# Token sums by halves, a first block in halves, no products that open banks early, and new ranks in the planner of a hybrid attention and pooling layer

## The chip, the cores and the metric

The kernel runs on one core of one Trainium2 chip. The metric is device microseconds (us) of one execution. The parts of the core are called by the profile's names: PE is TensorE, PEld its weight loads, DVE is VectorE, ACT is ScalarE, POOL is GpSimd, SP issues DMAs.

## The reference, cut to what matters

One decoder layer on 1024 tokens with 1024 channels, in float32:

```python
mod = silu(c) @ w_ada + b_ada
shift, scale, gate = jnp.split(mod, 3, axis=-1)
h = rms_norm(x, norm_w) * (1.0 + scale) + shift
proj = h @ w_in
u_pool, g_pool, q, k, v, g_attn, qi, ki, wi = jnp.split(proj, split_points, axis=-1)
pool_out = pool_mixer(u_pool, w_pool, pool_scale) * silu(g_pool)   # windows 2, 4, 8, 16
q = rope(rms_norm(q, q_norm_w)); k = rope(rms_norm(k, k_norm_w))
qi = rope(qi); ki = rope(ki)
score = sum over heads of relu(qi . ki) * wi, causal               # index scores
attn_out = attention of q over its 256 best scored keys * silu(g_attn)
x = x + gate * (concat([pool_out, attn_out]) @ w_out)
```

## The kernel before

The work is tiled by 128: 8 blocks of 128 channels, 8 tiles of 128 tokens. A float32 product of h with weights is made of three products of rounded parts: `hhi` with `wh`, `hhi` with `wl`, `hlo` with `wh`, where `wh` and `hhi` are the rounded values and `wl` and `hlo` what the rounding left.

The order on every engine is set when the kernel is built. `hybrid_layer` holds some 40 generators ("strands"), one for each piece of work; each yields an operation (`Op`), several to be issued together (`Group`), or the same operation on two or three engines to choose from (`Either`). `Flow.run` keeps a model of the engines' clocks, and issues at each step the operation whose modelled wait plus rank is least: the ranks stand in the table `EARLY` (for PE in `LAST`), `SAFE` adds a margin ahead of products of a strand, `_cost`, `HOP` and their like are the model's durations, `ROOM`, `KEEP`, `MIX`, `QK` and `IK` say how many buffers or banks a strand leaves to others. Since `Op.issue` (line 196) issues every instruction, every row of the profile has line 196, and rows are told apart by tiles.

The lead, which the change rewrites:

- `token_sums` (line 482) loads x as 8 blocks `xt`, squares each on ACT (`sq`), adds some of them on DVE, and sums the squares over channels with 64 products `m<-c,sq` of one column each, into eight columns of one bank.
- `token_scales` (line 534) takes the square root on ACT, the reciprocal on DVE, and spreads the result over the partitions by 8 PE transposes `m<-c,c` into two banks `ps_b`, copied by ACT to `rsb`.
- `modulations` (line 584) makes two DVE passes over 128x1024 weights (`wa`) for each block j; the sum of each goes through a small step, a DVE `TENSOR_SCALAR` on 128x1, that gives `gs` (the gear) and `mod_sb` (the shift).
- `h_block(j)` (line 608) makes xn, `hhi` on ACT and `hlo`. Block 0 takes xn on DVE in halves from `ps_b`; blocks 1 to 7 take it on POOL from `rsb`, and ACT applies gear and shift.
- `lead_line` (line 663) is PE's first long piece: for each j the index queries, three kinds of product, each with 512 and with 256 columns. It opens two banks with one float32 product each, `mm(acc..., ident, xt[7])`, the rows `m<-xt,c`.

After the lead come the key and value rows, then the steps of `ORDER`: a (gates), q (queries), m (pooling mixers); at "|" they wait for four finished score tiles. Beside these run the index scores, and then the selection of the 256 best keys by bisection: for tiles 2, 3 and 4 on DVE (31 steps; each step counts with one `junk` for each tile and moves the bound with `aq` and `xq`; `yq` is on POOL), for tiles 5, 6 and 7 on ACT (`ajunk`). Mixer g makes window sums `nx` from u, then u itself, which PE multiplies (`m<-u,c`), then `gp`, and its parts `mph` and `mpl` for the output projection. `attention` takes maxima `mx` of the products `m<-kT,qr` on DVE and goes on with exponentials, transposes and products; `project_pooled` and `project_attended` end the kernel.

Of the kernel before, what the change touches and what calls it, by code (L numbers as in the profile page):

```python
# [38 lines left out]
EARLY = {"main": 0.6, "fill": 0.4, "weights": 0.0, "evac": -1.0, "side": 0.2, "h": -0.2, "mods": -0.2,  # L39
         "select": -0.1, "scores": -0.6, "attend": -1.1, "late": 1.0, "kv": -0.3, "qi": -0.8, "pick": -0.6,  # L40
         "mix": -0.36, "rotated": -0.18, "query_loads": 0.01, "exps": -0.11, "score_sums": -1.13,
         "key_value_out": -0.58, "index_queries": -1.39, "norm": -2.29, "gate_loads": -0.03, "token_scales": -0.31,
         "gate_mods": 0.58, "unit": -0.41, "index_scores": -0.39, "lead_loads": 1.53, "out": -1.53, "lead_out": -0.72,
         "weight_loads": -0.1, "key_value_weights": -0.24, "main_line": 1.04, "output_line": 0.3, "turns": -1.82,
         "finish": -0.62, "index_keys": -0.9, "h_block": -0.1, "attention_keys": -0.68, "turned": -1.72,
         "h_blocks": -0.05, "gated": -1.24}
# [22 lines left out]
PW_POOL = 0.4  # L69
XO_POOL = 0.45  # L70
BACK = 0.5
SPAN = 0.5
# [1448 lines left out]
```

## Time and profile before

| | us |
|---|---|
| runs of the kernel | 533.91, 534.77, 534.86 (median 534.77) |
| profiled execution, its time | 535.14 |
| profiled execution, its span | 533.2 |
| PE busy | 510.2 (96%) |
| DVE busy | 427.3 (80%) |
| ACT busy | 376.4 (71%) |
| POOL busy | 160.5 (30%) |

The span runs from the first to the last instruction; what lies around it is 1.9 us. A busy share is a mean over stages: the table of stretches shows where an engine is full. A row of a timeline gives start, duration, engine, operation, out<-in, count, and in brackets the idle time just before it with the engine that ended it. Several rows of one kind that follow each other are one row with a count.

### The profile page before, as it was taken

The page shows a single profiled execution, that of the slowest core. Times are in us where ns is not written, and L with a number is a line of the kernel's source. Part 1 is how long each engine was busy: PE and PEld are TensorE (multiplying, and loading weights), DVE is VectorE, ACT ScalarE, POOL GpSimd, SP SyncE. Part 2 cuts the span into 40 slices and gives each one's busy share as a digit, 9 for nine tenths or more (in the row PEclk, how much of TensorE's full clock was granted, in tenths as well). Part 3 has the DMA queues.
Part 4 walks back from the last instruction along what each step waited for, and adds up shares of the span by engine and source line. Part 5 has one row for each costly group of instructions (what it writes and reads, how often), then busy time and mean ns, then how long its engine had stood idle before and what let it go on. Part 6 is the DMA issues. An engine that isn't in the chain of part 4 may idle for free.

```text
span 533.2 us, 7630 instructions
## 1 busy us (share of the span) xinstructions
PE 510.2 (96%) x2492; PEld 378.2 (71%) x2492; DVE 427.3 (80%) x895; ACT 376.4 (71%) x848; POOL 160.5 (30%) x173
## 2 busy tenths in 40 slices
PE   5969999999999999999999797999999999999997
PEld 5758899755657887878878575876585856636575
DVE  0699996699886899999999899798856999886142
ACT  6357731487878888999962789799999834796420
POOL 1298240000000345555246147243202423100000
PEclk9979999999999999999999798899999999999999
DMA  8995418202011111121110014465252723301044
GB/s 307 405 408 167 136 48 297 79 0 80 21 61 59 41 41 41 39 71 49 36 44 20 21 60 125 131 188 182 69 177 81 227 90 100 98 20 41 1 157 158
DMA packets 28023, 58.29 MB, mean 109 GB/s; under 512 B 3792, under 2 KB 7888, under 8 KB 27984
## 3 DMA queue, kind: packets, MB, share of 16 engines
q1 hardware_dynamic: 27984, 57.81, 31.8%
q8 instruction: 19, 0.31, 0.3%
q14 instruction: 20, 0.16, 0.1%
HBM read 47.32 MB, written 10.49 MB: 108 GB/s over the span
## 4 chain that ended last, share of the span: by engine, by line
PE 55%; DVE 31%; ACT 6%; issue 5%; DMA 1%; POOL 1%; SPq 0%; DVEq 0%; POOLq 0%
PE m L196 55%; DVE junk L196 9%; ACT ex L196 4%; DVE ex L196 3%; DVE selw L196 3%; DVE aq L196 2%; DVE nx L196 1%; DVE sw L196 1%; DVE xq L196 1%; DVE key L196 1%; DVE wa L196 1%; DVE u L196 1%; DVE hlo L196 1%; DVE qr L196 1%; DVE gp L196 1%
## 5 line engine op out<-in xcount | busy, mean ns | idle before, releaser
L196 PE MATMUL m<-hhi,wh 128*128 128x512 f32 (+1 forms) x320 | 120.8, 399 | 0.5 <-ACT hhi L196 0.5
L196 PE MATMUL m<-hlo,wh 128*128 128x512 f32 (+1 forms) x320 | 114.8, 383 | 4.5 <-DVE hlo L196 4.5
L196 PE MATMUL m<-hhi,wl 128*128 128x512 f32 (+1 forms) x320 | 115.7, 383 | 0.0
L196 ACT ACTIVATE ajunk<-key,xq 128x768 bf16<-128x768 uint16 (+2 forms) x93 | 96.4, 1037 | 4.9 <-DVE xq L196 3.6
L196 PEld LDWEIGHTS m<-hhi,wh 128*128 128x128 f32 x320 | 59.6, 191 | 21.0 <-issue 7.4
L196 POOL TENSOR_TENSOR wl<-ld,wh 128x512 fp32r<-128x512 f32 x40 | 61.6, 1542 | 33.8 <-ACT wh L196 15.3
L196 PEld LDWEIGHTS m<-hlo,wh 128*128 128x128 f32 x320 | 59.2, 190 | 16.9 <-DVE hlo L196 5.2
L196 DVE TENSOR_SCALAR_CACHE_REDUCE junk<-key,xq 128x384 bf16<-128x384 uint16 (+2 forms) x93 | 69.1, 743 | 2.2
L196 PEld LDWEIGHTS m<-hhi,wl 128*128 128x128 f32 x320 | 59.5, 191 | 12.9 <-issue 1.9
L196 ACT ACTIVATE ex<-ex,mx,c 128x256 f32<-128x256 f32 (+7 forms) x64 | 54.8, 858 | 2.2 <-DVE mx L196 2.1
L196 ACT ACTIVATE kt<-m 128x512 f32<-128x512 f32 (+1 forms) x80 | 38.0, 523 | 13.3 <-DVE score L196 9.5
L196 DVE SCALAR_TENSOR_TENSOR score<-kt,c,score 128x1024 f32<-128x1024 f32 (+5 forms) x42 | 39.9, 950 | 6.7 <-ACT kt L196 4.8
L196 PE MATMUL m<-kT,qr 64*128 64x512 f32 (+3 forms) x192 | 39.0, 515 | 3.5 <-DVE mx L196 3.5
L196 DVE CUSTOM_DVE_ANT_0 ex<-m,key 128x512 f32<-128x512 f32 (+1 forms) x48 | 30.9, 661 | 6.3 <-PE m L196 6.3
L196 PEld LDWEIGHTS m<-c,ex 128*128 128x128 f32 x288 | 31.7, 140 | 5.9 <-ACT ex L196 2.8
L196 PE MATMUL m<-c,ex 128*128 128x128 f32 x288 | 35.1, 275 | 0.8 <-ACT ex L196 0.8
L196 DVE SCALAR_TENSOR_TENSOR xo<-m,c,xo 128x512 f32<-128x512 f32 x23 | 17.0, 740 | 22.6 <-PE m L196 22.3
L196 PEld LDWEIGHTS m<-kT,qr 64*128 64x128 f32 x192 | 18.2, 188 | 22.6 <-issue 12.2
L196 PE MATMUL m<-pw,vrow 128*64 128x512 f32 x144 | 33.5, 601 | 0.0
L196 PE MATMUL m<-kiT,qix 64*128 64x512 f32 (+3 forms) x160 | 32.2, 532 | 0.0
L196 POOL TENSOR_SCALAR_AFFINE_SELECT score<-score 128x128 f32<-128x128 f32 x6 | 3.1, 510 | 91.1 <-PE m L196 46.5
L196 ACT CAST wh<-ld 128x512 fp32r<-128x512 f32 x35 | 21.4, 617 | 11.2 <-PE m L196 11.2
(182 smaller groups left out, 1050.7 us busy)
## 6 DMA issues: line engine op xcount, KB each, us to landing
wa<-wada SPq DMA_DIRECT2D x24, 512.0 KB, 7.5
ld<-wet SPq DMA_DIRECT2D x16, 512.0 KB, 3.3
ld<-wout SPq DMA_DIRECT2D x24, 256.0 KB, 2.8
xo<-xT SPq DMA_DIRECT2D x16, 256.0 KB, 3.3
y_d<-xo SPq DMA_DIRECT2D x16, 256.0 KB, 2.3
xo<-y_d SPq DMA_DIRECT2D x16, 256.0 KB, 3.0
outT<-xo SPq DMA_DIRECT2D x16, 256.0 KB, 2.1
xt<-xT SPq DMA_DIRECT2D x7, 512.0 KB, 6.9
```

What stands on the lines that cost most here:

```text
L196: self.fn(*self.args, **self.kw)
```

## The change

1. The token sums go into two banks of four columns, one for each half of the tokens, the half 512 to 1023 first. The last block of x is loaded and squared in this order too. Square root, reciprocal and transposes are made for each half.
2. The two banks are no longer opened with `m<-xt,c`; `WARM`, an empty list before, and its bank are gone.
3. Block 0 has a generator of its own, `first_block`; each half waits for its own transposes, and PE's products wait for (block, half) instead of the block.
4. The small steps of the modulation are strands `gear` and `shift` that the planner puts on ACT or DVE. POOL makes the constant `bnw` that ACT's form needs.
5. Ranks, margins, model durations, buffer limits and `ORDER` have new values, and ranks can be given for one instance of a strand (`"gated 7"`).

The diff, cut to its core:

```diff
-ORDER = "a2 a0 a1 q1 q2 | q0 m1 q3 m3 m2 m0 a3"
+ORDER = "a0 a1 a2 q2 q1 q0 m1 q3 m3 m2 m0 | a3"
-WARM = [()] * 8
...
-         "finish": -0.62, "index_keys": -0.9, "h_block": -0.1, "attention_keys": -0.68, "turned": -1.72,
+         "finish": -1.36, "index_keys": -2.21, "h_block": -0.1, "attention_keys": -1.2, "turned": -1.63,
+         "h_blocks": -0.84, "gated": -1.42, "modulations": -0.22, "low": -0.59, "gear": 0.31, "attention": -0.51,
...
-SCALED = (0,)
+SCALED = ()
-WKM = 4
+WKM = 2
-QK = 4
-IK = 4
+QK = 2
+IK = 2
-MIX = 4
-KEEP = 6
+MIX = 5
+KEEP = 7
-XN_AHEAD = 2
+XN_AHEAD = 1
-FAVOUR = {"DVE": 0.122, "ACT": -0.13, "POOL": 0.013}
+FAVOUR = {"DVE": 0.125, "ACT": 0.148, "POOL": 0.005}
...
     def spawn(self, gen, kind="side"):
-        s = [gen, EARLY.get(gen.__name__, EARLY[kind]), None, kind]
+        name = gen.__name__
+        n = self.spawned[name] = self.spawned.get(name, 0) + 1
+        s = [gen, EARLY.get(f"{name} {n}", EARLY.get(name, EARLY[kind])), None, kind]
...
-            for c in ([slice(0, 512), slice(512, 1024)] if j == NT - 1 else [slice(0, 1024)]):
+            for c in ([slice(512, 1024), slice(0, 512)] if j == NT - 1 else [slice(0, 1024)]):
                 yield SP.dma_start(t[:, c], xT[j][:, c])
...
-                        yield mm(ps_r[:, b:b + 1], t[:, b * P:(b + 1) * P], ones, j == SUMS[0] and b == 0,
-                                 j == NT - 1 and b == NT - 1)
+                                yield mm(tab["sums"][h][:, b:b + 1], t[:, o:o + P], ones,
+                                         h not in started, j == NT - 1 and b == 3)
...
     def token_scales():
-        yield A.activation(rs, tab["sums"], AF.Sqrt, scale=1.0 / 1024.0, bias=eps_sb)
-        yield V.reciprocal(rs, rs)
+        for h, r in enumerate((rs[:, 4:8], rs[:, 0:4])):
+            yield A.activation(r, tab["sums"][h], AF.Sqrt, scale=1.0 / 1024.0, bias=eps_sb)
+            yield V.reciprocal(r, r)
+            ps = yield bank()
+            yield Group([PE.transpose(ps[:, b * P:(b + 1) * P], r[:, b:b + 1].to_broadcast([P, P]), ident)
+                         for b in range(4)])
+            rsbs.append(ps)
...
-            yield V.tensor_scalar(gs[:, j:j + 1], m, bada_sb[:, 8 + j:9 + j], nw_sb[:, j:j + 1],
-                                  op0=OP.add, op1=OP.mult)
+            flow.spawn(gear(j, g), "mods")
...
+    def gear(j, g):
+        yield Either(A.activation(gs[:, j:j + 1], g, AF.Identity, scale=nw_sb[:, j:j + 1], bias=bnw[:, j:j + 1]),
+                     V.tensor_scalar(gs[:, j:j + 1], g, bada_sb[:, 8 + j:9 + j], nw_sb[:, j:j + 1],
+                                     op0=OP.add, op1=OP.mult))
+    def shift(j, m):
+        b = bada_sb[:, j:j + 1]
+        yield Either(A.activation(m, m, AF.Identity, bias=b), V.tensor_scalar(m, m, b, None, op0=OP.add))
...
+    def first_block():
+        def low(n, c):
+            yield V.scalar_tensor_tensor(lo[:, c], xn[:, c], m, hi[:, c].bitcast(F32), op0=OP.add, op1=OP.subtract)
+        for n, c in enumerate((slice(512, 1024), slice(0, 512))):
+            yield lambda: len(rsbs) > n and 0 in geared
+            yield V.scalar_tensor_tensor(xn[:, c], xt[0][:, c], g, rsbs[n], op0=OP.mult, op1=OP.mult)
+            yield lambda: 0 in modded
+            yield A.activation(hi[:, c], xn[:, c], AF.Identity, bias=m)
+            flow.spawn(low(n, c), "h")
...
-        for _ in range(2):
-            acc[len(acc), 0] = yield bank()
-            yield mm(acc[len(acc) - 1, 0], ident, xt[NT - 1][:, :512], True, True)
...
-                if k == 2:
-                    yield lambda: j in hlo
+                yield lambda: (j, c) in (lo_in if k == 2 else hi_in)
```

Three places in the order of the instructions are shown; every row of the kernel after has line 209, where `Op.issue` now stands.

DVE in the lead, from the last sums to block 1's `hlo`, before (c_92 is the token scale, c_89 and c_90 are shift and gear; `hlo_284` is block 1's):

```order
L196 SCALAR_TENSOR_TENSOR wa_207,c_89<-wa_207,m 128x1024
L196 RECIPROCAL c_92<-c_92 128x8
L196 TENSOR_SCALAR c_90<-c_89,c_78,c_77 128x1
L196 SCALAR_TENSOR_TENSOR wa_209,c_89<-wa_209,m 128x1024
L196 SCALAR_TENSOR_TENSOR xn_255<-xt_107,c_90,m 128x512
L196 TENSOR_SCALAR c_89<-c_89,c_78 128x1
L196 SCALAR_TENSOR_TENSOR wa_212,c_89<-wa_212,m 128x1024
L196 SCALAR_TENSOR_TENSOR xn_255<-xt_107,c_90,m 128x512
...
L196 SCALAR_TENSOR_TENSOR wa_219,c_89<-wa_219,m 128x1024
L196 TENSOR_SCALAR c_90<-c_89,c_78,c_77 128x1
L196 SCALAR_TENSOR_TENSOR hlo_273<-xn_255,c_89,hhi_272 128x512
```

and after (c_93 is the token scale now):

```order
L209 RECIPROCAL c_93<-c_93 128x4
L209 SCALAR_TENSOR_TENSOR wa_209,c_89<-wa_209,m 128x1024
L209 RECIPROCAL c_93<-c_93 128x4
L209 SCALAR_TENSOR_TENSOR wa_211,c_89<-wa_211,m 128x1024
L209 TENSOR_SCALAR c_90<-c_89,c_78,c_77 128x1
L209 SCALAR_TENSOR_TENSOR xn_243<-xt_108,c_90,m 128x512
L209 SCALAR_TENSOR_TENSOR wa_214,c_89<-wa_214,m 128x1024
L209 SCALAR_TENSOR_TENSOR xn_243<-xt_108,c_90,m 128x512
L209 SCALAR_TENSOR_TENSOR wa_219,c_89<-wa_219,m 128x1024
L209 SCALAR_TENSOR_TENSOR hlo_245<-xn_243,c_89,hhi_244 128x512
L209 SCALAR_TENSOR_TENSOR wa_221,c_89<-wa_221,m 128x1024
L209 SCALAR_TENSOR_TENSOR hlo_245<-xn_243,c_89,hhi_244 128x512
```

A reciprocal of four columns now stands ahead of the first `wa`, all small steps but the first have left this stretch of DVE, and each half of block 0's `hlo` comes one `wa` sooner. On PE the rows `m<-xt,c` between the sums, the transposes and block 0 are gone, and nothing else moved there.

ACT where the magnitudes of tiles 2, 3 and 4 (`kt`, which the first DVE count needs) and the evacuations of the queries (`st`) meet the first steps of ACT's bisection (`ajunk`, `aq`), before:

```order
L196 ACTIVATE ajunk_1492,c0q_241_1466<-score_1217 128x640
L196 ACTIVATE st_1510<-m 128x512
L196 ACTIVATE qr_1438<-m,c_95 128x512
L196 ACTIVATE ajunk_1502,cq_251_1485<-key_87,xq_250_1483 128x896
L196 ACTIVATE kt_1535<-score_1303,sgnq_243_1468 128x384
L196 ACTIVATE ajunk_1516,cq_251_1485<-key_88,xq_250_1483 128x1024
L196 ACTIVATE aq_260_1538<-cq_251_1485,kcq_199_1248 128x1
L196 ACTIVATE kt_1542<-score_1303,sgnq_243_1468 128x512
L196 ACTIVATE aq_260_1538<-cq_251_1485,kcq_199_1248 128x1
L196 ACTIVATE st_1559<-m 128x512
L196 ACTIVATE qr_1438<-m,c_95 128x512
L196 ACTIVATE kt_1567<-score_1217,sgnq_243_1468 128x640
```

and after:

```order
L209 ACTIVATE ajunk_1480,cq_243_1451<-key_87,xq_242_1449 128x896
L209 ACTIVATE ajunk_1497,c0q_247_1469<-score_1220 128x640
L209 ACTIVATE ajunk_1499,cq_243_1451<-key_88,xq_242_1449 128x1024
L209 ACTIVATE aq_257_1510<-cq_243_1451,kcq_197_1240 128x1
L209 ACTIVATE st_1520<-m 128x512
L209 ACTIVATE qr_1443<-m,c_96 128x512
L209 ACTIVATE kt_1525<-score_1306,sgnq_249_1471 128x384
L209 ACTIVATE aq_257_1510<-cq_243_1451,kcq_197_1240 128x1
L209 ACTIVATE kt_1537<-score_1306,sgnq_249_1471 128x512
L209 ACTIVATE kt_1548<-score_1220,sgnq_249_1471 128x640
L209 ACTIVATE aq_257_1510<-cq_243_1451,kcq_197_1240 128x1
```

Two `ajunk` (896 and 1024 columns) now stand ahead of the first evacuation, and the second evacuation behind the three `kt`.

DVE around the u of the last mixer (`u_2745` before, `u_2762` after; PE multiplies it) and the bisection for tiles 2 to 4, before:

```order
L196 TENSOR_SCALAR junk_3014,cq_658_2996<-key_85,xq_651_2969 128x640
L196 TENSOR_TENSOR nx_3003<-nx_3003,c_98 128x16
L196 TENSOR_TENSOR aq_666_3029<-cq_658_2996,kcq_244_1469 128x3
L196 SCALAR_TENSOR_TENSOR xq_667_3030<-aq_666_3029,yq_668_3031 128x3
L196 TENSOR_SCALAR junk_3051,cq_673_3050<-key_83,xq_667_3030 128x384
L196 SCALAR_TENSOR_TENSOR u_2745<-nx_3003,u_2745 128x1024
L196 TENSOR_SCALAR junk_3053,cq_673_3050<-key_84,xq_667_3030 128x512
```

and after, down to the first maximum of attention (`ISA ex,mx`):

```order
L209 TENSOR_SCALAR junk_3063,cq_678_3045<-key_85,xq_672_3019 128x640
L209 SCALAR_TENSOR_TENSOR u_2762<-nx_3031,u_2762 128x1024
L209 TENSOR_TENSOR aq_685_3067<-cq_678_3045,kcq_250_1472 128x3
...
L209 TENSOR_TENSOR aq_713_3162<-cq_702_3127,kcq_250_1472 128x3
L209 CAST mph_3176<-gp_2245 128x1024
L209 CAST mph_3180<-gp_2763 128x1024
L209 SCALAR_TENSOR_TENSOR xq_714_3163<-aq_713_3162,yq_715_3164 128x3
L209 ISA ex_3175,mx_2437<-m,mask_82 128x128
```

The count of `junk` rows ahead of this u goes from 79 to 84, and ahead of the first maximum from 87 to 90, one whole step of the bisection; two casts `mph` that ACT made before stand there too.

## Rows read from the trace of the kernel before

**Rows 1.** The page's first lines: the span, and busy time, share and count of each engine.

```profile
span 533.2 us, 7630 instructions
PE 510.2 (96%) x2492; PEld 378.2 (71%) x2492; DVE 427.3 (80%) x895; ACT 376.4 (71%) x848; POOL 160.5 (30%) x173
```

**Rows 2.** Busy time of each engine in stretches of the span (from:to, length, PE, PEld, DVE, ACT, POOL, granted PE clock as a share of full speed, DMA share, GB/s).

```profile
36.00:75.00 39.00, 39.00 (x223) 34.92 (x223) 37.94 (x53) 24.48 (x35) 25.48 (x12) 0.95 0.47 162
...
250.00:300.00 50.00, 47.09 (x204) 37.66 (x202) 48.71 (x101) 33.88 (x74) 21.07 (x28) 0.99 0.13 42
```

**Rows 3.** What PE waited for, whole span: us in total, times, longest us.

```profile
PE m L196 <- DVE hlo L196: 4.5, 2, 2.8
PE m L196 <- DVE mx L196: 3.5, 2, 1.8
PE m L196 <- DVE u L196: 2.8, 1, 2.8
```

**Rows 4.** Timeline of PE in the lead, from the token sums to block 4's last products.

```profile
7.39 13.79 PE L196 MATMUL m<-c,sq 128*128 128x1 f32 x64 [0.52 <-ACT sq L196]
21.03 2.05 PE L196 MATMUL m<-xt,c 128*128 128x512 f32 x2
...
26.87 1.19 PE L196 MATMUL m<-hhi,wh 128*128 128x512 f32 x4 [0.49 <-ACT hhi L196]
...
36.66 1.91 PE L196 MATMUL m<-hhi,wh 128*128 128x512 f32 x4
...
42.29 1.09 PE L196 MATMUL m<-hhi,wh 128*128 128x512 f32 x4
...
53.49 1.56 PE L196 MATMUL m<-hlo,wh 128*128 128x512 f32 x8
```

**Rows 5.** Timelines of DVE, ACT and POOL in the lead; the last DVE row is block 4's `hlo`.

```profile
17.12 1.22 DVE L196 SCALAR_TENSOR_TENSOR wa<-wa,m 128x1024 f32<-128x1024 f32 x1
...
21.51 0.20 DVE L196 RECIPROCAL c<-c 128x8 f32<-128x8 f32 x1 [3.17 <-ACT c L196]
21.70 0.27 DVE L196 TENSOR_SCALAR c<-c,c,c 128x1 f32<-128x1 f32 x1
...
24.83 0.75 DVE L196 SCALAR_TENSOR_TENSOR xn<-xt,c,m 128x512 f32<-128x512 f32 x1 [1.72 <-PE m L196]
...
30.43 1.14 DVE L196 SCALAR_TENSOR_TENSOR hlo<-xn,c,hhi 128x512 fp32r<-128x512 f32 x1
...
32.64 2.94 DVE L196 SCALAR_TENSOR_TENSOR hlo<-xn,c,hhi 128x512 fp32r<-128x512 f32 x1
...
50.74 1.98 DVE L196 TENSOR_TENSOR hlo<-xn,hhi 128x1024 fp32r<-128x1024 f32 x1
21.21 0.27 ACT L196 ACTIVATE c<-m,c 128x8 f32<-128x8 f32 x1 [5.67 <-PE m L196]
...
26.09 0.72 ACT L196 ACTIVATE hhi<-xn,c 128x512 fp32r<-128x512 f32 x1
32.69 5.13 POOL L196 TENSOR_TENSOR xn<-xt,rsb 128x1024 f32<-128x1024 f32 x2
```

**Rows 6.** Timeline of ACT at the end of the index scores, from the first evacuation of a query to the last magnitude.

```profile
171.37 0.58 ACT L196 ACTIVATE st<-m 128x512 f32<-128x512 f32 x1
...
173.96 1.13 ACT L196 ACTIVATE ajunk<-key,xq 128x1024 bf16<-128x1024 uint16 x1
...
177.12 0.82 ACT L196 ACTIVATE kt<-score,sgnq 128x640 f32<-128x640 f32 x1
```

**Rows 7.** Timelines of DVE and PE: the first count on DVE, an `aq`, the u of the third mixer and the first maximum; then PE's first product with that u.

```profile
178.62 0.61 DVE L196 TENSOR_SCALAR_CACHE_REDUCE junk<-key,xq 128x384 bf16<-128x384 uint16 x1
...
296.74 0.16 DVE L196 TENSOR_TENSOR aq<-cq,kcq 128x3 f32<-128x3 f32 x1
...
298.71 1.22 DVE L196 SCALAR_TENSOR_TENSOR u<-nx,u 128x1024 f32<-128x1024 f32 x1
...
327.01 0.29 DVE L196 CUSTOM_DVE_ANT_0 ex<-m,mask 128x128 f32<-128x128 f32 x1
299.98 2.08 PE L196 MATMUL m<-u,c 128*128 128x512 f32 x2 [2.78 <-DVE u L196]
```

**Rows 8.** Groups of instructions between 178 and 327 us, one row for each shape: count, busy us, mean ns of one, idle us before.

```profile
L196 POOL TENSOR_TENSOR wl<-ld,wh 128x512 fp32r<-128x512 f32 x21 | 30.6, 1459 | 23.9 <-issue 10.5 <-ACT wh L196 7.4 <-DVE xq L196 5.1
L196 DVE TENSOR_SCALAR_CACHE_REDUCE junk<-key,xq 128x640 bf16<-128x640 uint16 x29 | 25.4, 877 | 0.7
...
L196 DVE TENSOR_SCALAR_CACHE_REDUCE junk<-key,xq 128x384 bf16<-128x384 uint16 x29 | 17.7, 611 | 0.8
L196 DVE TENSOR_TENSOR aq<-cq,kcq 128x3 f32<-128x3 f32 x28 | 14.8, 527 | 0.6
...
L196 POOL TENSOR_TENSOR qr<-qr,cos 128x1024 f32<-128x1024 f32 x3 | 8.2, 2749 | 5.9 <-DVE sw L196 4.5 <-DVE xq L196 1.4
...
L196 DVE SCALAR_TENSOR_TENSOR xq<-aq,yq 128x3 f32<-128x3 f32 x27 | 7.8, 288 | 1.9
...
L196 POOL TENSOR_TENSOR nx<-nx 128x1022 f32<-128x1022 f32 x2 | 3.9, 1944 | 3.7 <-DVE nx L196 3.7
...
L196 DVE TENSOR_TENSOR nx<-nx 128x1020 f32<-128x1020 f32 x2 | 2.4, 1215 | 0.0
...
L196 DVE CAST wh<-ld 128x512 fp32r<-128x512 f32 x3 | 1.3, 419 | 0.0
```

More of the change, by code (lines that the diff above doesn't have):

```diff
@@ L36 @@
 ROOM = {"b": 36, "ld": 2, "st": 3, "wh": 4, "wl": 4, "kt": 2, "sg": 2, "selw": 1, "m": 8}
[L39 to L44, printed above, removed]
-         "finish": -0.62, "index_keys": -0.9, "h_block": -0.1, "attention_keys": -0.68, "turned": -1.72,
-         "h_blocks": -0.05, "gated": -1.24}
@@ L48 @@
-SELECT = -0.461
-LAST = {"main": 0.12, "fill": 0.129, "scores": 0.008}
-SAFE = {"side": 1.0, "unit": 0.1, "query_norms": 0.67, "rotated": 0.7, "norm": 0.45, "weight_loads": 0.1}
-SCALED = (0,)
+EARLY = {"main": 0.6, "fill": 0.4, "weights": 0.0, "evac": -1.0, "side": 0.2, "first": -0.4, "h": -0.2,
+         "mods": -0.2, "select": -0.1, "scores": -0.6, "attend": -1.1, "late": 1.0, "kv": -0.3, "qi": -0.8,
+         "pick": -0.6, "mix": -0.36, "rotated": 0.33, "query_loads": 0.4, "exps": -0.11, "score_sums": -1.15,
+         "key_value_out": -1.08, "index_queries": -0.81, "norm": -2.67, "gate_loads": 0.24, "token_scales": -0.31,
+         "gate_mods": 0.13, "unit": -0.41, "index_scores": 0.2, "lead_loads": 1.49, "out": -1.53, "lead_out": -0.86,
+         "weight_loads": 0.25, "key_value_weights": 0.11, "main_line": 0.99, "output_line": -0.32, "turns": -1.71,
+         "finish": -1.36, "index_keys": -2.21, "h_block": -0.1, "attention_keys": -1.2, "turned": -1.63,
+         "h_blocks": -0.84, "gated": -1.42, "modulations": -0.22, "low": -0.59, "gear": 0.31, "attention": -0.51,
+         "maxima": -0.99, "score_relus": -0.66, "gated 7": -1.16, "gated 3": -1.23, "index_queries 2": -1.03,
[3 rows of a table added]
+         "norm 6": -2.43, "out 11": -1.67, "shift 2": -1.16, "out 9": -1.89, "query_norms": -0.01, "gear 2": 0.79,
[4 rows of a table added]
@@ new lines @@
+SELECT = -0.222
+LAST = {"main": 0.519, "fill": 0.114, "scores": 0.229, "attend": -0.005, "evac": 0.202, "qi": -0.049,
+        "side": -0.228}
+SAFE = {"side": 1.0, "unit": 0, "query_norms": 0.23, "h_block": 0, "rotated": 0.36, "query_loads": 0,
+        "norm": 0.45, "weight_loads": 0, "key_value_out": 0, "turned": 0.26, "finish": 0, "index_keys": 0.17,
+        "main_line": 0, "output_line": 0, "gate_mods": 0.41, "selection": 0.38, "low": 0, "maxima": 0,
+        "attention": 0.36, "lead_out": 0, "score_relus": 0.77, "products": 0, "key_value_weights": 0.27,
+        "attention_keys": 1.72, "out": 0.05, "scores": 0, "mix": 1.55, "main": 0.28}
@@ L67 @@
 AGE = 0.37
[L69 to L72, printed above, removed]
-QK = 4
-IK = 4
+PW_POOL = 0.299
+XO_POOL = 0.298
+BACK = 0.456
+SPAN = 0.347
+QK = 2
+IK = 2
 FK = 2
 PK = 0
-MIX = 4
-KEEP = 6
+MIX = 5
+KEEP = 7
 FLY = 2
@@ L611, in h_block @@
         scaled = j in SCALED
[L612 removed]
         if scaled:
[L614 to L624 removed]
+            yield lambda: j in geared
+            yield V.scalar_tensor_tensor(xn, xt[j], gs[:, j:j + 1], tab["rsb"], op0=OP.mult, op1=OP.mult)
+        else:
+            yield G.tensor_tensor(xn, xt[j], tab["rsb"], op=OP.mult)
         flow.drop(xt[j])
[L626 removed]
+        yield lambda: j in modded and j in geared
         hi = yield big(F32R, s="hhi")
```

107 lines of the change are left out of this document (55 added, 52 removed), and 7 rows, old and new, of the table EARLY.

## The prediction

> **What bounds the kernel now.** [...] First the page's shares: PE is busy 510.2 of 533.2 us [rows 1], so a gain has to come out of the 23 us in which it isn't, or out of stretches in which it runs at the lower clock. Then what PE waits for: DVE's `hlo` twice in the lead (4.5), one u of a mixer (2.8), two maxima of attention (3.5) [rows 3]; behind DVE each time. Then the stretches: DVE is busy 37.94 of 39 us in the lead, and 48.71 of 50 at 250 to 300 [rows 2]. So two places are DVE-paced, the lead up to 54 us and the bisection from the first count at 178.62 to the first maximum at 327.01 [rows 7]; between them PE is full, and a gain of the lead is carried on without loss only if DVE's queue in the second place is shifted by as much. [...]
>
> **The lead.** The 64 sum products set the start: 13.79 us from 7.39, 0.215 each, end 21.2, and the one square root starts there [rows 4, 5]. With halves, the first half's last products end some 8 of these (1.7 us) sooner, so square root (0.27) and reciprocal (0.20) of the first half are done near 20.0, DVE makes its first `wa` to 21.2, then the second reciprocal to 21.7, the second `wa` (1.22 long, 1.14 from start to start) to 22.9, the gear (0.27), and xn of a half, 0.75, to 23.8; `hhi` with 0.72 gives PE its first product near 24.7, where it had it at 26.87 [rows 4, 5]: 2.2 sooner. Taking the `wa` away from ahead of the reciprocal costs nothing on PE's path but makes DVE idle from the last squares' sum to the reciprocal, which is one `wa`, 1.14, in this DVE-paced stretch; it is in the sum that follows.
>
> What sets the end of the lead is DVE's queue. From the second reciprocal at 21.7 to block 4's `hlo` the changed order has 13 `wa` at 1.14 (14.8), one gear (0.2), two xn halves at 0.68 (1.4), two `hlo` halves and four whole `hlo` at some 1.9 (7.6, the last row of DVE in [rows 5] less the overlap). [...] From 2.3 to 5.9 for both, the sum ends between 48.0 and 51.6. Before, the same block's `hlo` ended at 52.7 and PE used it at 53.49 [rows 4, 5]. So PE can be 5.5 to 1.9 ahead there; I take the middle, **3.7 us**. The 15 small steps that leave DVE for the lead (some 0.15 each from start to start, 2.3) are in this sum already; on ACT they cost some 0.28 each, 4.2, and ACT is busy only 24.48 of 39 us there [rows 2], so they are hidden. If that cover were gone, each would lie in the chain from `wa` to `hhi`, 0.1 a block.
>
> The removed `m<-xt,c` (2.05 and 1.79 us of PE time, of which the first is in [rows 4]) lay in PE's wait for the scales and cost nothing before; their removal gains nothing by itself. What they did for the clock is a rival below.
>
> **The end of the scores.** The first DVE count needs the last `kt`. From the first evacuation at 171.37 to that `kt`'s end at 177.94 ACT takes 6.57 us [rows 6]. The changed order puts two `ajunk` (1.13 and some 1.03) ahead of that evacuation, and the second evacuation with its scaling (some 1.05) behind the `kt`: 6.57 - 1.13 - 1.03 - 1.05 = 3.4, a shift by 3.2. It is worth nothing if ACT, full there, is late with the evacuation itself. DVE also loses some four `wl` to POOL before it. I take **3.5** in all, with 0 as the other end.
>
> **The bisection stretch.** I counted DVE's rows from the first `junk` to the first maximum: 213 before, 228 after. The additions: one whole step more before the maximum (`junk` 0.877 and 0.611 with some 0.74 between them, `aq` 0.527, `xq` 0.288: 3.0) and one more pair `aq`, `xq` (0.8); three `nx` that POOL had (1.215 each, 3.6); two `mph` casts of 1024 columns (twice 0.419 each, 1.7); small ones that nearly cancel (some 0.8) [rows 8]. Sum +9.9. Against it stands what DVE now waits for: `aq` works on three columns and takes 527 on the mean, but 0.16 at 296.74 [rows 7, 8], `xq` 288. Their excess over 0.16 is 28 x 0.367 + 27 x 0.128 = 13.7 us, some 17 with the wide operations, all beside POOL's operations with two inputs; of their some 47 us (`wl` 30.6, rotations 8.2, `nx` 3.9 [rows 8] and two more) three `nx` and one rotation product of 2.7, about 9 us, go. A fifth to a quarter of 17 is 3.8. Net **+6.1**, with +9.9 (no relief) and +3 (the relief twice as large) as ends. [...]
>
> The u of the third mixer suffers most: PE reaches it 12 products (2.7 us) sooner in its own order, and DVE's u is later in DVE's queue; PE waits there, as it did at 299.98 [rows 7], and for longer.
>
> **The sum.** From the first maximum on PE is full but for short waits, its work is the same to 1 us by count, and the order of the tail hardly moves. So the end moves as the first maximum does: -3.7 - 3.5 + 6.1 = -1.1 on the profiled execution of 535.14, 534.0; that execution lies 0.37 above the median of the runs, so I predict **533.7**.
>
> **Rivals.**
> - A, the forecast: DVE's longer queue takes back most of what the lead gives. With the ends of its terms taken apart, 531.5 to 536.
> - B: DVE is relieved by more than I count, so u and maxima come in time. Then the lead's 3.7 stays, and some of the 2.8 at u and of the 3.5 at the maxima [rows 3] goes: -3.7 to -6.5, 531.1 to 528.3. I put it at 529.8. For it speaks that POOL, idle often, has room for what DVE waits for; against it that DVE's queue gets 15 rows longer.
> - C, the slower side: the queue's growth comes without relief, +9.9, since DVE is 97% busy at 250 to 300 [rows 2] and each `junk` is ahead of a u or a maximum. -3.7 - 3.5 + 9.9 = +2.7, 537.4. It decides where growth passes 7.2.
> - D: without the wide products ahead of it, PE begins block 0 at the lower clock. Before, the four first products took 1.19 at 26.87, the upper level, after `m<-xt,c`; at the lower level such a row took 1.91 [rows 4]. A block of 24 products would take up to 4 us longer, part of it in PE's waits for `hlo`; with 2.2 left over, 535.9. [...]
>
> **How the numbers follow.** A 0.43, B 0.27, C 0.18, D 0.12. The predicted time is A's. 0.2% is 1.07 us, about what a measurement of this kernel can tell from no change. A's own range lies on both sides: 0.21 faster, 0.14 within, 0.08 slower. B is faster; C slower; D 0.02, 0.06 and 0.04. That makes faster 0.50, same 0.20, slower 0.30. The range goes from B's far end to C: 528.5 to 537.4.
>
> **What the profile after would show.** Right: PE's first `hhi` product near 24.7; block 4's `hlo` products near 49.8; the key and value rows 3 to 4 us sooner; DVE's first count near 171.4; a wait of 3 to 7 us for the third mixer's u; the first maximum near 326. Wrong: the lead gains under 2 (D, if its products take 1.9 past 30 us); `aq` means stay above 0.5 (C) or fall below 0.35 (B); PE without a wait for u (B). A wait of a new kind in the tail, above 2 us, would make the sum wrong altogether.

## The result and the profile after

The changed kernel takes 526.63 us (median of 4 runs, 526.09 to 526.86), the kernel before took 534.34 beside it (532.85 to 534.86). The ratio is 0.9859, 95% interval [0.9836, 0.9881]. Forecast was 533.7 with a range from 528.5 to 537.4: right in sign, too slow by 7.1 us and outside the range. The profiled execution took 526.09 us, 9.05 less than that of before. The kernel before does not always take the same time: beside the experiments 60 executions of it lie between 528.6 and 535.2, with medians of 530.5 to 532.0, so the four here and the profiled one are toward its slow end, and beside `after_again`, the same kernel as after, the gain is 4.5 us.

The first lines of its page; line 209 is where every instruction is issued now:

```profile
span 524.0 us, 7622 instructions
PE 504.4 (96%) x2488; PEld 376.8 (72%) x2488; DVE 419.3 (80%) x880; ACT 372.7 (71%) x847; POOL 180.1 (34%) x192
```

Against [rows 1], PE and DVE are each busy some 6 to 8 us less, POOL 20 more. Stretches, in the columns of [rows 2]:

```profile
36.00:75.00 39.00, 38.16 (x229) 34.28 (x228) 37.88 (x42) 25.07 (x50) 31.28 (x13) 1.00 0.56 193
250.00:300.00 50.00, 49.04 (x208) 38.67 (x207) 48.70 (x108) 31.27 (x70) 16.30 (x26) 1.00 0.11 37
```

DVE is as full as before in both, yet in the second PE is busy 49.04 us, where it had 47.09. What PE waited for:

```profile
PE m L209 <- DVE mx L209: 4.5, 4, 2.1
...
PE m L209 <- DVE u L209: 1.4, 3, 0.6
PE m L209 <- DVE hlo L209: 1.2, 2, 0.8
```

Of the three waits of [rows 3], that for `hlo` (4.5) is mostly gone, that for u (2.8 at once) is half in sum and 0.6 at most, and that for the maxima has grown by 1. The lead on PE, as in [rows 4]:

```profile
24.60 2.08 PE L209 MATMUL m<-hhi,wh 128*128 128x512 f32 x4 [1.77 <-ACT hhi L209]
26.47 1.91 PE L209 MATMUL m<-hhi,wl 128*128 128x512 f32 x4
...
30.20 1.67 PE L209 MATMUL m<-hlo,wh 128*128 128x512 f32 x8 [0.80 <-DVE hlo L209]
31.71 1.09 PE L209 MATMUL m<-hhi,wh 128*128 128x512 f32 x4
...
47.11 1.56 PE L209 MATMUL m<-hlo,wh 128*128 128x512 f32 x8
...
54.20 1.21 PE L209 MATMUL m<-hhi,wl 128*128 128x512 f32 x4 [0.41 <-POOL wl L209]
...
58.67 0.50 PE L209 MATMUL m<-hlo,wh 128*128 128x512 f32 x1 [0.43 <-DVE hlo L209]
62.52 0.32 PE L209 MATMUL m<-wkh,hhi 128*128 128x328 f32 x1
```

Block 0 starts 2.27 us sooner and its first four products take 2.08, where before had 1.19, which only shortens the wait at 30.20; from block 1 on four take 1.09 (granted clock 1.00 from 31.7 to 36). That block 0 ran at a clock of 0.50 is an estimate, from the 1.91 that four such products took at a granted clock of 0.50 in before (36.66, [rows 4]): the trace of after has no clock record ahead of 28.4 us. Block 4's `hlo` products come at 47.11 (53.49 before), and after two short waits the key and value rows at 62.52, 5.0 sooner than the 67.48 of before.

The clock tells the two executions apart as well. In that of before, PE's granted clock stands at 0.50 of full speed three times, each time in or behind waits of PE: for `hlo`, for the u and for maxima. In that of after it does so once, behind the waits for maxima. These are all the stretches at 0.50 from 32 us to PE's end, three of before, then one of after:

```profile
32.95:39.78 6.83, 4.14 (x12) 3.47 (x13) 6.83 (x7) 2.48 (x2) 6.83 (x3) 0.50 1.03 410
299.19:306.02 6.83, 6.04 (x11) 3.49 (x11) 5.44 (x14) 3.15 (x11) 0.23 (x1) 0.50 0.12 37
329.91:336.74 6.83, 5.53 (x14) 4.01 (x15) 6.66 (x31) 4.54 (x13) 2.26 (x2) 0.50 0.47 145
321.94:328.77 6.83, 6.33 (x16) 3.95 (x15) 6.11 (x30) 6.20 (x15) 2.98 (x3) 0.50 0.31 106
```

How far the clock falls behind one and the same wait differs between executions. Behind the wait of 2.78 us for the third mixer's u it is at 0.50 for 6.83 us in before, for 3.41 in `old_lead_steps_on_act` and `new_lead_old_rest`, which have the same order there, and not at all in `before_13_steps`. The times of the 60 executions go with it: 535.1 to 535.2 at a mean granted clock of 0.979 to 0.981, 528.6 to 529.8 at 0.990 to 0.994.

Where the 9.2 us of PE's end lie, from the timelines of the two profiled executions (us from the start of the span):

| | before | after | moved by | added there |
|---|---|---|---|---|
| PE's first product of the key and value rows | 67.48 | 62.52 | -4.96 | -5.0 |
| DVE's first count | 178.62 | 172.85 | -5.77 | -0.8 |
| first maximum of attention | 327.01 | 320.07 | -6.94 | -1.2 |
| end of PE's last product with `mph` | 410.32 | 401.83 | -8.49 | -1.55 |
| PE's end | 529.37 | 520.17 | -9.20 | -0.7 |

The forecast had -3.7, -3.5, +6.1 and nothing for the last two.

How much of each row belongs to the change shows beside other traces with before's order in the same stretch. The key and value rows come at 67.02 in `before_13_steps` and at 65.64 in `before_sums_on_dve`, so the lead's gain is 3.1 to 5.0. From the first count to the first maximum before takes 148.4 us, but `old_lead_steps_on_act` and `new_lead_old_rest` take 147.1 and 147.2, and six traces with after's order 147.2 to 147.4: the -1.2 of that row is the longer fall of the clock behind the u in this one execution, and against the other two nothing is left of it. (The instructions are the same; one DVE row, `gp` at 306.35 in before, waits 1.47 us for PE, and 0.20 and 0.22 in the other two.) The rows for the tail hold: from the first maximum to PE's end before's order takes 201.7 to 202.4 in three traces and after's 199.6 to 201.0 in six.

The end of the scores on ACT, as in [rows 6]:

```profile
167.77 1.15 ACT L209 ACTIVATE ajunk<-key,xq 128x1024 bf16<-128x1024 uint16 x1
...
169.10 0.57 ACT L209 ACTIVATE st<-m 128x512 f32<-128x512 f32 x1
...
170.84 1.44 ACT L209 ACTIVATE kt<-score,sgnq 128x512 f32<-128x512 f32 x2
```

From the evacuation `st` to the last `kt` are 3.2 us, as worked out (3.4), but `st` itself comes only 2.27 sooner than before, with the lead 4.96 ahead: the `ajunk` in front of it are not free on a full ACT (busy 10.19 of the 10.8 us ahead of 167.8). Then the bisection, as in [rows 7] and [rows 8]; the last two rows are the groups of 178 to 327 us:

```profile
172.85 0.61 DVE L209 TENSOR_SCALAR_CACHE_REDUCE junk<-key,xq 128x384 bf16<-128x384 uint16 x1
...
290.82 1.22 DVE L209 SCALAR_TENSOR_TENSOR u<-nx,u 128x1024 f32<-128x1024 f32 x1
...
320.07 0.28 DVE L209 CUSTOM_DVE_ANT_0 ex<-m,mask 128x128 f32<-128x128 f32 x1
292.09 1.99 PE L209 MATMUL m<-u,c 128*128 128x512 f32 x4 [0.63 <-DVE u L209]
L209 DVE TENSOR_TENSOR aq<-cq,kcq 128x3 f32<-128x3 f32 x29 | 9.9, 341 | 0.5
L209 DVE SCALAR_TENSOR_TENSOR xq<-aq,yq 128x3 f32<-128x3 f32 x28 | 7.1, 252 | 1.7
```

The `aq` fell from 527 to 341 ns on the mean, and PE's wait for the third mixer's u from 2.78 to 0.63, where the forecast had 3 to 7. To have one number for such delays, I took each DVE row of the stretch against the shortest row of the same shape and summed what is over 0.08 us: this **excess** is 17.6 us before (10.5 of it in `aq`, 3.6 in `xq`; 11.4 beside a `wl` of POOL, in 15 rows of several kinds) and 9.8 after (5.5, 2.65; 7.7 in 11 rows). DVE's busy time in the stretch is 140.90 before and 140.85 after, though 15 rows of work were added: the additions are there, and something of equal size went away.

### The profile page after: what moved, and what is told of

It is laid out like the page before. It is cut to its first block, busy times and chain, and to the rows that moved or that the text cites. A ratio compares the mean times of both kernels' runs of the same rounds, so it can differ in the third digit from the quotient of the medians.

```text
span 524.0 us, 7622 instructions
## 1 busy us (share of the span) xinstructions
PE 504.4 (96%) x2488; PEld 376.8 (72%) x2488; DVE 419.3 (80%) x880; ACT 372.7 (71%) x847; POOL 180.1 (34%) x192
## 4 chain that ended last, share of the span: by engine, by line
PE 71%; DVE 20%; issue 3%; ACT 0%; DVEq 0%
PE m L209 71%; DVE junk L209 6%; DVE wa L209 3%; DVE hlo L209 2%; DVE selw L209 2%; DVE nx L209 1%; DVE aq L209 1%; DVE xq L209 1%; DVE ex L209 1%; DVE u L209 1%; DVE gp L209 1%; DVE wkl L209 1%; DVE key L209 1%; DVE mpl L209 0%; DVE xn L209 0%
## 5 line engine op out<-in xcount | busy, mean ns | idle before, releaser
L209 PE MATMUL m<-hhi,wh 128*128 128x512 f32 (+1 forms) x320 | 119.1, 394 | 1.8 <-ACT hhi L209 1.8
L209 PE MATMUL m<-hlo,wh 128*128 128x512 f32 (+1 forms) x320 | 113.6, 380 | 1.2 <-DVE hlo L209 1.2
L209 POOL TENSOR_TENSOR wl<-ld,wh 128x512 fp32r<-128x512 f32 x46 | 69.3, 1508 | 60.4 <-ACT wh L209 45.8
L209 ACT ACTIVATE kt<-m 128x512 f32<-128x512 f32 (+1 forms) x80 | 37.6, 524 | 13.9 <-DVE score L209 10.8
L209 POOL TENSOR_SCALAR wh<-ld 128x512 fp32r<-128x512 f32 x23 | 16.2, 704 | 62.4 <-PE m L209 59.3
L209 PE MATMUL m<-c,ex 128*128 128x128 f32 x288 | 33.7, 273 | 1.8 <-DVE mx L209 1.8
L209 PE MATMUL m<-kiT,qix 64*128 64x512 f32 (+3 forms) x160 | 33.9, 538 | 0.0
L209 PEld LDWEIGHTS m<-kiT,qix 64*128 64x128 f32 x160 | 16.2, 186 | 15.2 <-issue 9.0
```

What stands on the lines that cost most here:

```text
L209: self.fn(*self.args, **self.kw)
```

## The experiments

Two questions had to be told apart: is the gain that of the lead, or of the order behind it; and does the excess set the stretch of the bisection, or do the rows behind it just close up? Every kernel but the first two holds its order of issue as a list, taken from before or after, so that one thing moves and the rest stays. Ratios are against the kernel before, run beside each with medians of 530.5 to 532.0; stretches are those of the table.

**1 and 2. One half of the change each.** The first has the new lead with before's ranks, the second the old lead with the new ranks; both leave the order to the planner. Of the first's edit, the smallest lines (the tables of ranks go with them; the second's edit is the reverse, in before):

```diff
-ORDER = "a0 a1 a2 q2 q1 q0 m1 q3 m3 m2 m0 | a3"
+ORDER = "a2 a0 a1 q1 q2 | q0 m1 q3 m3 m2 m0 a3"
...
-SELECT = -0.222
+SELECT = -0.461
...
-HOP = 0.096
+HOP = 0.103
```

> The new lead (sums by halves, first block in halves, no opening products, small steps on either engine) with every rank, margin, cost and limit of the kernel before, so that the planner lays the rest out anew. The kernel after gained 5.0 us by the start of the key and value rows, and 9.2 at the end of its span. Theory 1 (both parts carry: the lead's gain goes through to the end, the ranks relieve DVE in the bisection and spare the fall of the clock at the third mixer's u): the key and value rows 3 to 5 sooner than before's 67.5, time near 530. Theory 2 (the lead alone, ranks neutral): near 527. Theory 3 (as forecast, DVE's queue in the bisection takes the lead's gain back unless the ranks change it): 533 to 535.

> The lead of the kernel before (whole sums, two opening products, small steps on DVE) with all ranks, margins, costs, limits and the order of steps of the kernel after. Theory 1: the key and value rows near 67, time near 531. Theory 2: 534 to 535. Theory 3: near 528, since the ranks are what made the gain.

The first took 565.98 us, ratio 1.0643 [1.0607, 1.0678]: the planner makes a different program of it, which waits everywhere (`hlo` 6.2, maxima 6.0, `ex` 4.9, `st` 3.4). It says that the ranks fit one lead, and nothing on the lead's price. The second took 533.18, ratio 1.0037 [1.0019, 1.0055]: its key and value rows come at 70.38, 2.9 later than before (six waits for `hlo`, 5.5), but from there to PE's end are 458.9 us, against 461.9 before and 457.65 after. So behind the lead the ranks gain some 3 (the two other traces with before's order there have 460.2 and 460.5, four with after's 457.2 to 458.3).

**3 and 4. Taking the lead apart.** The products that open banks go back in; or the halves of block 0 are loaded and scaled in the other order.

```diff
 def token_scales / main_line (banks_opened)
+        for _ in range(2):
+            acc[len(acc), 0] = yield bank()
+            yield mm(acc[len(acc) - 1, 0], ident, xt[NT - 1][:, :512], True, True)
 (late_half)
-            for c in ([slice(512, 1024), slice(0, 512)] if j == NT - 1 else [slice(0, 1024)]):
+            for c in ([slice(0, 512), slice(512, 1024)] if j == NT - 1 else [slice(0, 1024)]):
```

> The kernel after, its order of issue written out as a list and kept, with the two opening products back where they stood before, one ahead of the transposes of the scales and one behind them. If they only keep the clock up: block 0's first four products take 1.2 us instead of 2.08, but wait for hlo all the same, and the time is within 0.6 of 526.6. If they stand in the way of the transposes: the first product of block 0 comes up to 2 us later than 24.6 and the time is 1 to 2 longer. If the removal cost the clock (rival D): 1 to 3 us shorter.

> The kernel after, same order of issue on every engine, but the last block of x is loaded, squared and summed with the lower half first, so that the half whose scales are made first is the one whose sums end last: sums by halves without their gain in time. If the early half sets the lead's start: first reciprocal near 21.2 instead of 19.6, the key and value rows 1.3 to 1.7 later, and the time 1.2 to 1.8 longer. If DVE's queue or POOL's sets the lead anyway: less than 0.6 longer.

`banks_opened` took 527.77 us, ratio 0.9929 [0.9901, 0.9957]. Its lead on PE:

```profile
20.72 2.05 PE L253 MATMUL m<-xt,c 128*128 128x512 f32 x2
22.57 1.91 PE L253 MATMUL m<-c,c 128*128 128x128 f32 x8
...
26.25 1.44 PE L253 MATMUL m<-hhi,wh 128*128 128x512 f32 x4
27.53 1.08 PE L253 MATMUL m<-hhi,wl 128*128 128x512 f32 x4
...
31.86 1.66 PE L253 MATMUL m<-hlo,wh 128*128 128x512 f32 x8 [2.30 <-DVE hlo L253]
```

Block 0's first products then take 1.44 and 1.08 instead of 2.08 and 1.91, as rival D had it, and it buys nothing: the first opening product stands ahead of `m<-c,c`, the token scales that `xn` needs, so what hangs on them is later by 1.65 (first `hhi` product 26.25), the wait for `hlo` grows from 0.80 to 2.30, and the 1.7 stay to PE's end (+1.78). `late_half` took 527.67, ratio 0.9921 [0.9892, 0.9950]: first product +1.2, end +0.95. A delay of the lead reaches the end whole in the first and by two thirds in the second (1.42 at the key and value rows, 0.95 at the end).

**5. The new lead, and from the key and value rows on the order of before.** The list is after's up to those rows and before's behind them.

> The lead of the kernel after, instruction by instruction on every engine, up to the key and value rows, and from there the order of the kernel before, both written out as a list and kept. This parts the lead's gain from the ranks', which a new planning of the new lead with the old ranks could not (its plan was another one, 566 us). Theory 1 (the lead's gain is carried in full, since DVE's first count follows PE's score products): key and value rows near 62.5, first count near 173.5, a stretch from there to the first maximum of 148.4 as before, the third mixer's wait 2.8 and the fall of the clock behind it as before, time 4.5 to 5.5 under before. Theory 3 (DVE's queue takes it back): less than 2 under before.

528.02 us, ratio 0.9907 [0.9871, 0.9944]. The key and value rows come at 62.57, PE's end 6.65 sooner than before; the wait for u is 2.8 as before, the excess 17.3. So the lead's 5 us are carried without the new order behind it; the new order adds some 2.5 in the profiled executions and 1.4 by the medians, which were not taken side by side; its ratio and that of `after_again`, 0.9900 [0.9876, 0.9924], are not apart.

**6 to 8. Steps of modulation.** In the list of after the gears and shifts go from ACT to DVE; in that of before they go from DVE to ACT.

```diff
 (steps_on_dve: the engine of each gear and shift in the list)
-ACT
+DVE
 (old_lead_steps_on_act)
-        yield V.tensor_scalar(m, m, b, None, op0=OP.add)
+        yield A.activation(m, m, AF.Identity, bias=b) if act else V.tensor_scalar(m, m, b, None, op0=OP.add)
```

> The kernel after, same order, with the 15 small modulation steps that ACT got put back on DVE. By the forecast's sum they take 0.12 to 0.19 each of DVE's queue, 2.3 us by block 7. If DVE's queue sets the lead: key and value rows 1 to 2 us later than 62.5 and the time longer by as much. If PE sets it from block 1 on (it ran blocks 1 to 5 without a wait): less than 0.6.

> The kernel before, its order of issue written out and kept, with the 16 small modulation steps on ACT instead of DVE and nothing else of the change. With these steps back on DVE the kernel after lost 6.0 us by the key and value rows. Theory L1 (the steps are what paces the lead: two DVE rows for each block and the collisions of hlo with POOL's xn that follow): key and value rows 2 to 4 us sooner than 67.5, hlo's mean under 1.6 us instead of 1.70, time 2 to 4 under before. Theory L2 (it takes the early half scales and the steps together): less than 1.

> The kernel after, unchanged, on the chip of this call, for a comparison beside the same runs of before. It gave 526.63 against 534.34 where it was first timed; before has lain between 528.6 and 535.2 since. Expected 526 to 527, and its milestones within 0.2 us of the first profile's.

`steps_on_dve` took 531.93 us, ratio 0.9998 [0.9973, 1.0024]: the whole gain is gone. Its key and value rows come at 68.53, 6.0 later than after's; PE's waits:

```profile
PE m L253 <- DVE hlo L253: 5.4, 5, 2.3
```

The 15 small steps are some 2.3 us of DVE at the forecast's 0.15 each; the rest lies in `hlo`, 1.855 us on the mean for a whole one against 1.391 in after (seven of them, 3.2), and 3.5 us for the two halves against 2.5: DVE, later by the steps, meets POOL's `xn` again (the first half, 27.05 to 29.83, beside an `xn` from 26.90 on). `old_lead_steps_on_act` took 533.08, ratio 1.0013 [0.9988, 1.0038]: in the old lead the same move gives nothing. There PE's wait only changes its name:

```profile
PE m L241 <- ACT hhi L241: 4.2, 2, 2.2
```

So steps and halves have to come together. `after_again` is after from its list, unchanged: 526.90, ratio 0.9900 [0.9876, 0.9924], with every place of the table within 0.4 us.

**9 and 10. Does DVE's queue set the stretch of the bisection?** DVE makes 13 of its 16 steps for tiles 2 to 4, in before and in after.

```diff
-            for b in range(nbits - 1, -1, -1):
+            last = 3 if nbits == 16 and not act else 0
+            for b in range(nbits - 1, last - 1, -1):
```

> The kernel before, order kept, without the last three of the 16 steps of the second bisection of tiles 2 to 4 on DVE (it leaves these low bits of the thresholds out; 9 junk, 3 aq, xq and yq, some 8 us of DVE's queue ahead of the first maximum). If DVE's queue sets the stretch, as forecast: first maximum 5 to 8 us sooner than 327.0, PE's waits for mx gone, time 4 to 8 under before. If PE sets it: the waits for mx (3.5) go and the clock's fall behind them, 3 to 6 at most. If neither: less than 1.

> The order of after without the last three of DVE's sixteen steps for tiles 2 to 4 (the three lowest bits of their thresholds are left out), as it was done to before. If DVE's queue still sets the stretch in after as it did in before, the stretch falls from 147.2 by some 4 to 5 us, to 143, and the end with it. If DVE was relieved so far that PE sets it now, it falls by under 2 us.

Before: 527.93 us, ratio 0.9924 [0.9899, 0.9949]; the stretch falls from 148.4 to 143.3, the wait for the maxima from 3.5 to 1.1, PE's end is 7.0 us sooner. Not all of that is the edit's: 0.5 lie in the lead and 2.9 behind the wait for the u, ahead of the steps left out, where the clock did not fall this time. The edit's own part is some 3.6, and 3.5 by the medians (531.40 and 527.93). After: 525.18, ratio 0.9890 [0.9859, 0.9921]; the stretch falls from 147.2 to 144.6, but PE's end by only 0.6, and the wait for the maxima stays (4.7). So DVE's queue set the end in before, by those 3.5. In after it hardly does: PE's own first product of attention does not move (316.98 against 316.90), and what DVE gives at the first maximum is lost again by the next ones.

**11 and 12. The three sums `nx`.** Their engine in the list is swapped: to POOL in after, to DVE in before.

> The kernel after, same order, with three window sums nx (1022, 1016 and 1022 columns) moved from DVE back to POOL, where the kernel before had them. By the count of the forecast DVE is relieved by 3.6 us and the time falls by up to 3. [...]

> The kernel before, order kept, with the three window sums nx that POOL has moved to DVE, the one move of the bisection stretch taken alone. By the forecast's price: DVE gets 3.6 us more and the first maximum comes 2 to 4 later than 327.0, time 1 to 4 over before. [...]

In after, on POOL: 526.63 us, ratio 0.9894 [0.9860, 0.9928]; excess 11.2 instead of 9.8, first maximum 1.0 later, no difference in time beyond the interval. In before, on DVE: 532.31, ratio 1.0020 [1.0000, 1.0039]; the excess falls from 17.6 to 13.9, the stretch from 148.4 to 147.6. Against `old_lead_steps_on_act` and `new_lead_old_rest`, where the clock fell behind the u for 3.41 us as it did here, the stretch is 0.5 longer. The forecast had priced this move at +3.6. The three rows are on DVE now, and it costs next to nothing, since the excess fell by 3.7: DVE had waited about as long for them on POOL.

**13. POOL's `wl` out of the way of `aq`.** In the list of after, nine `wl` go behind the next `yq`.

> The kernel after with one change in POOL's order alone: the nine wl products beside which an aq or xq of the bisection on DVE stood too long (0.3 to 1.25 us instead of 0.16) are put behind the next yq, so that they run beside junk, which has one input. [...] If DVE's waits are hidden (PE sets the stretch): aq's mean falls and the time stays within 0.7 of 526.6. If wl is then late for PE: longer.

527.14 us, ratio 0.9899 [0.9865, 0.9933]: no gain. The excess of `aq` fell to 4.7 and of `xq` from 2.65 to 0.33, but that of `mpl` and `qsl` rose, and the sum with it, from 9.8 to 11.2. The delays move from row to row.

**14 and 15. POOL's `wl` made short.** Before and after in their own orders, with the low part replaced by a copy of `wh`: the low parts of these weights are left out of the result, and only the times are of use.

```diff
-                      G.tensor_tensor(lo, src, hi.bitcast(F32), op=OP.subtract))
+                      G.tensor_scalar(lo, hi.bitcast(F32), 1.0, 1.0, op0=OP.mult, op1=OP.mult))
```

> The order of before, with one operation changed: each `wl` that POOL makes is a copy of `wh` (one input) and not the difference of `ld` and `wh` (two inputs), so the low parts of these weights are left out of the result. Theory P (DVE's waits for POOL's operations with two inputs were a part of what set the stretch from the first count to the first maximum, and the changed kernel has fewer of them): the excess of DVE's rows in the stretch falls from 17.6 to some 6 us, and the stretch from 148.4 to some 143 us, where PE, full but for its waits, ends the gain; from the key and value rows to the end 461.9 becomes 455 to 458. Theory R (the rows behind such a wait close up with it, the waits are not what sets the stretch): the stretch stays within 1 us of 148.4.

> The order of after, with the same one operation changed (the low parts of POOL's weights left out). Theory P: the excess falls from 9.8 to some 2, less than it falls in before, and the stretch from 147.2 to 143 to 145, so that after is ahead of before by its lead alone, 5 to 6 us. Theory R: the stretch stays within 1 us of 147.2.

Before: 523.75 us, ratio 0.9866 [0.9831, 0.9901]. Groups of its stretch (178 to 318.6 us):

```profile
L241 POOL TENSOR_SCALAR wl<-wh 128x512 fp32r<-128x512 f32 x21 | 14.0, 665 | 27.4 <-ACT wh L241 13.2 <-DVE wh L241 10.5 <-DVE xq L241 2.8
L241 DVE TENSOR_TENSOR aq<-cq,kcq 128x3 f32<-128x3 f32 x28 | 9.2, 329 | 0.6
L241 DVE SCALAR_TENSOR_TENSOR xq<-aq,yq 128x3 f32<-128x3 f32 x27 | 5.9, 218 | 1.9
```

One `wl` takes 665 ns, where it took 1459 [rows 8], and `aq`, a DVE row on which nothing was changed, goes from 527 to 329. The excess falls to 7.8, the stretch from 148.4 to 140.4, and PE comes to the third mixer's u without a wait; the clock does not fall there, and its mean is 0.993 where it was 0.981. After: 522.16, ratio 0.9839 [0.9811, 0.9867]; excess 4.0, stretch 144.2. So POOL's `wl` cost the stretch 3.0 us after, and before 8.0 against this execution, 6.7 against the two with the shorter fall of the clock behind the u, and some 5 against `before_13_steps`, without a fall there (its DVE rows are 2.9 ahead of before's at the last one that both have in order). Theory P stands and R falls: even 3.0 is beyond its 1 us. With short `wl` PE's end in after is only 3.8 ahead of that in before (519.44 and 515.62; 1.6 by the medians), less than the 4.6 between their key and value rows: behind the lead the new order gains nothing then, as far as one profile of each tells. Its gain there is that it suffers less from these rows.

## Why the prediction was wrong

**The lead, -3.7 forecast, -5.0 measured (3.1 to 5.0 beside other traces): its first marks right, what sets the rest wrong.** The first half's reciprocal came at 19.64 (20.0), the first product at 24.60 (24.7). But DVE's queue down to block 4's `hlo` did not set the end of the lead. In before that `hlo` was ready at 52.72 [rows 5], and PE took it 0.8 later, behind rows of its own: from block 0's second `hlo` half to the key and value rows PE is full.

```profile
35.64:67.48 31.84, 31.84 (x172) 27.76 (x173) 30.78 (x48) 21.89 (x26) 19.69 (x10) 0.94 0.55 192
```

The forecast set DVE's end after against PE's use before, and so counted these 0.8 as gain. What PE gained is the end of its last long wait, 30.20 for 35.64, and block 1's first products at a granted clock of 1.00 instead of 0.50 (1.09 us for four, 1.91 before): block 4's products were 6.4 sooner, past the far end of 5.5, and two waits of 0.4 with what follows them gave 1.4 back. The 2.3 to 5.9 us that the sum has for block 0's two `hlo` halves were an estimate, twice the 1.14 and twice the 2.94 of [rows 5], and no run shows the far end: they took 4.1 in before, 3.5 in `steps_on_dve`, 1.9 in `before_sums_on_dve` and in after 2.5, near the cheap end. A whole one took 1.39, because POOL's `xn` was the one to wait (3.05 on the mean, 2.46 before): the `hlo` begun at 31.21 took 1.21, the `xn` begun at 31.27 beside it 3.44. That removing the opening products gains nothing was wrong for the new lead: there it is worth 1.7 (`banks_opened`). The small steps that I had as hidden work on ACT are indeed hidden there; kept on DVE they cost 6.0 (`steps_on_dve`), more than twice their own length.

**The end of the scores, -3.5 forecast, -0.8 measured.** The step that fails is "two `ajunk` ahead of that evacuation": I subtracted their time from the span between evacuation and end, and the evacuation was late by nearly as much. The text named this condition and its end at 0; I took the other end.

**The bisection, +6.1 forecast, -1.2 to nothing measured: the step that failed.** I added rows at their full length (+9.9) and took off "a fifth to a quarter of 17", 3.8, for the delays that go away. The step that fails is the +9.9. With short `wl`, where no fall of the clock lies in the stretch, before needs 140.4 us and after 144.2: the longer queue, with all that it changes but these rows, is worth **+3.8**. Part of that error is shown alone: moving the three `nx` measured -0.8 in before, +0.5 beside the traces of like clock, instead of +3.6, since on POOL they cost DVE as much in delays. The 3.8 taken off was about right: what `wl` costs fell by **5.0** (8.0 to 3.0) against the profiled before, by 3.7 and by some 2 against the others. So the sum is -1.2 in the profiled pair and about 0 beside the traces with the shorter fall. The wait for the third mixer's u, forecast to grow to 3 to 7 us, fell to 0.63, and the fall of the clock behind it, which the sum put at nothing, went with it (granted clock 1.00 there in after). The runs show that POOL's rows hold DVE's up: `aq` fell by 198 ns from one change on POOL (`wl` of 665 ns instead of 1459, `before_one_input`), and in before `aq`, 0.16 at 296.74, ends at 323.72 beside a `wl` that ends at 323.70, and `xq` at 324.72 beside `mph`, a row of POOL with one input that ends at 324.71:

```profile
322.92 0.80 DVE L196 TENSOR_TENSOR aq<-cq,kcq 128x3 f32<-128x3 f32 x1
323.83 0.89 DVE L196 SCALAR_TENSOR_TENSOR xq<-aq,yq 128x3 f32<-128x3 f32 x1
322.41 1.29 POOL L196 TENSOR_TENSOR wl<-ld,wh 128x512 fp32r<-128x512 f32 x1
323.67 1.04 POOL L196 TENSOR_SCALAR mph<-gp 128x1024 fp32r<-128x1024 f32 x1
```

Nine DVE rows were still held up beside the 665 ns copies, which have one input too. So the time of such rows of POOL belongs in the count, and my tally of 47 us, of rows with two inputs, had none of it.

**The tail, nothing forecast, -2.25 measured.** "The order of the tail hardly moves" was no ground for its time. The step of the bisection that the sum added ahead of the first maximum is gone from behind it, and the sum took nothing off there. In the 50 us behind the first maximum, before and after, DVE is busy 4.3 us less and PE 1.3 more:

```profile
327.01:377.01 50.00, 47.82 (x232) 35.11 (x232) 43.64 (x133) 45.96 (x129) 21.53 (x21) 0.93 0.53 163
320.07:370.07 50.00, 49.15 (x236) 35.82 (x238) 39.39 (x123) 42.90 (x119) 22.57 (x22) 0.93 0.50 158
```

That the one brings the other was not isolated, nor was the rest of the 2.25.

**Rivals.** B was the right one in kind: its marks, `aq` below 0.35 (0.341) and PE with hardly a wait for the third mixer's u (0.63), are there. It was priced by the waits of PE at u and maxima alone, so that even its far end, 528.3 (528.5 in the range), was too slow: it left the lead's and the tail's terms as they were. Luck has a part in the size of the miss: beside the faster executions of before the gain is 4.5, which B's far end, 6.5, covers. A and C fell with the +9.9. D's slower products came (2.08 instead of 1.19) and cost nothing that these rows show, since the next products wait for `hlo` anyway; `banks_opened`, with 1.44 there, is the slower one. With A's sum wrong, the even chances for and against a gain were wrong too.

**What stays open.** The tail's 2.25; why `wl` holds up 15 rows of DVE before and 11 after (which one of the new ranks does it was not tried); why the clock falls for 6.83 us, for 3.41 or not at all behind one and the same wait; and that short `wl` also free POOL earlier, so that a part of the 8.0 and 3.0 may be POOL's own time and not DVE's waits.

## What to carry to other kernels

Before pricing a row that moves from GpSimd to VectorE, look at what VectorE's neighbouring rows take beside it and beside nothing: a three-column operation whose mean is 527 ns and that takes 160 at its best in the rows shown says that the move may be free (here +3.6 forecast, -0.8 and +0.5 measured). Where VectorE is full, one short run with GpSimd's long rows made short tells what they cost (here 3.0 to 8.0 us of the stretch), better than any tally. Small steps on a paced engine can cost more than their length (here 6.0 us for 15 of them) when they shift its rows onto another engine's. And before a stretch of one profile is set against that of another, compare TensorE's granted clock in the two: here 1.3 us of a stretch were an execution's, and not the order's.

## What was not expected of the hardware

The same order of instructions does not take the same time in its lead. `before_sums_on_dve` has before's lead instruction for instruction, yet its key and value rows come at 65.64 and not 67.48:

```profile
L239 DVE TENSOR_TENSOR hlo<-xn,hhi 128x1024 fp32r<-128x1024 f32 x7 | 12.6, 1805 | 0.0
L239 DVE SCALAR_TENSOR_TENSOR hlo<-xn,c,hhi 128x512 fp32r<-128x512 f32 x2 | 1.9, 936 | 0.0
L239 POOL TENSOR_TENSOR xn<-xt,rsb 128x1024 f32<-128x1024 f32 x7 | 21.2, 3036 | 1.7 <-ACT rsb L239 1.7
```

The halves of `hlo` take 0.94 us on the mean there, against 1.14 and 2.94 in [rows 5], and POOL's `xn` 3.04 where before has 2.46: as far as these rows show, which of the two is first is decided by little, and the other takes longer. The kernel before was measured between 528.6 and 535.2 us in all its runs, and after only between 525.8 and 527.1. The fall of the clock behind PE's waits, long in some executions and missing in others (6.83 us, 3.41 or none behind the third mixer's u), goes with that spread (mean granted clock 0.979 at 535.2, 0.994 at 528.6); whether the meeting of `hlo` and `xn` adds to it was not isolated.
